# Later places in TensorE's queue for second blocks of norms, attention's transposes, one filter's products and the memory's transposes

## The chip, the cores and the metric

One core of a Trainium2 chip runs the whole program. The time is that of one execution on the device, in microseconds (us); the kernel before took 1537.53 us in the median of three runs (1534.23 to 1537.7). TensorE (PE) multiplies and transposes, VectorE (DVE) and ScalarE (ACT) do elementwise work, GpSimd (POOL) some squares, and SyncE's queue (SP) brings the weights in.

## The reference

Two networks of depth 2 run one behind the other on 256 tokens of 1024 numbers, in fp32. Each layer of the first is a mixer, a cross attention over a memory of 256 tokens and a feed-forward part, with a layer norm behind each:

```
for l in range(DEPTH):
    mix = hybrid_mixer(h, w_in[l], conv_w[l], ..., w_out[l], cos, sin)
    h = layer_norm(DEEPNORM_ALPHA * h + mix, ln1_g[l], ln1_b[l])
    h = layer_norm(DEEPNORM_ALPHA * h + cross_attention(h, mem, cq_w[l], ckv_w[l], co_w[l]),
                   ln2_g[l], ln2_b[l])
    h = layer_norm(DEEPNORM_ALPHA * h + swiglu(h, ffn_wi[l], ffn_wo[l]), ln3_g[l], ln3_b[l])
```

The mixer has two branches of one projection: a gated recurrence, and attention of 16 query heads over 2 key heads in a window of 128 tokens, with a sink per head:

```
r = jax.nn.sigmoid(... w_rg ... + b_rg)
i = jax.nn.sigmoid(... w_ig ... + b_ig)
log_a = -LRU_C * r * softplus(-lru_lambda)
h = associative_scan(combine, (exp(log_a), sqrt(-expm1(2 * log_a)) * (i * xc)))
y_rnn = h * gelu(gr)
probs = softmax(concatenate([scores, sink]))[..., :-1]
merged = sigmoid(g_rnn) * (y_rnn @ w_br_rnn) + sigmoid(g_attn) * (y_attn @ w_br_attn)
```

The second network has a differential attention and long convolutions by FFT, whose filters come from a small sine network times a decay: `h = (a @ w_out) * exp(-t * abs(deltas))`. Two layers have two filters each.

## The kernel before, in words

Every weight is used once. SyncE's queue streams them in chunks of 1 MB (`raw`, three buffers). A chunk is used in two halves; of each half ACT makes a rounded copy `wh` (L231) and DVE the remainder `wl` (L233), in four buffers each, and each product is the sum of three matmuls (`wh` with the high part of the activations, `wl` with it, `wh` with their low part). The activations are split in the same way (L360 on ACT, L361 on DVE). An `fm` tile gives features on partitions and is 48 matmuls of 256 columns; `tm` and `ff` give tokens on partitions, 512 columns a matmul; `gate` tiles, of 12 matmuls, are the two gate products of the recurrence. These four are called bulk work here: 98% of PE's time is kept by them and by the side work that stands between them.

Side work is written as coroutines. PE's and SP's queues stand in the order in which the program issues instructions. It keeps a clock of its own, `self.t`, that each matmul advances; a coroutine that says `yield L["sc"]` is not asked again until that clock has gone on by `L["sc"]` (in ns), and its next step is then issued at the next point between bulk work where such steps are let in (each 12 matmuls of 256 columns, or 6 of 512). So the table `L` sets, for each step, how much bulk work stands ahead of it on PE; it is no wait on the chip. DVE's, ACT's and POOL's queues are ordered by a scheduler, which sees PE's order, the dependences and a priority per coroutine (`PRI`). Each engine then runs its queue strictly in order.

The side work that matters:

- Attention (`swa_co`, L676 to 730). For four groups (block of 128 tokens, key head): scores `sc`; on DVE mask and maximum (L688, L692); on ACT exponentials in place (`scs`, L699), their sums' reciprocal spread out (`rbs`, L707); then `yield L["sc"]`; transposes `pt`, copied from PSUM by ACT (L717); `rb` and `y`; and a product on DVE (L729) and a split. Groups of the first block take scores in two parts. `scs` tiles have five buffers.
- The gates (L758 on). ACT takes each `gate` tile out of PSUM by two sigmoids (`r`) or two tanhs (`ig`), all L782. `fm` and `gate` tiles share a PSUM pool of four buffers; `tx`, `tm`, `sc`, `pt`, `rb`, `y` and `ff` another of four.
- The recurrence (`rnn_co`): 16 exponentials and tanhs (L803, L805), a square root (L815), gelu of the other branch (`gr`, L817), scans on DVE (L821 to L826).
- A norm's result is transposed by block of 128 tokens, eight `tx` each from `t` (written last at L601): `ln_co` issues the first block after 500 ns, the second after `L["ln<layer><norm>"]`.
- The memory's transposes (`tx` from `mem`), at the start.
- `vec_co`: transposes of small vectors, copied by DVE (L547; L1201 in a part that it calls), and rates of the recurrence (L550 to L572).
- Filters: `filter_mul` multiplies (`fh`, L1325 on) by a weight `fwo` that ACT and DVE split (L1308, L1309). Three of the four filters are late; the one at layer 0, index 1 is not.

ACT holds one set of functions at a time; where the next instruction's function is in another set, the queue has an ACT_TABLE_LOAD.

Of the kernel before, what the change touches and what calls it, by code (L numbers as in the profile page):

```python
# [38 lines left out]
LATE = ((0, 0), (1, 0), (1, 1))  # L39
# [1 line left out]
NSLOT = 29  # L41
NTMP = 8
NKEEP = 5
PRI = {'filter_dft': -60, 'cross_co': 60, 'filter_end': 30, 'rnn_co': 30, 'mlp_co': 60}

L = dict(
    vec=6000, flt=12000, fh=1200, fe=18000, prep=15000, mlp=7500, sc=11000, rnn=7000, rnn2=11700,
    pt=3000, tx=0, spec=6000, sp0=3000, sp1=5000, sp2=5000, sp3=5000, ds=9000, dn=8960, do=5500,
    z=12000, cn=1000, cp=2000, ln_0=500, ln01=3500, ln02=5500, ln03=6000, ln11=5000, ln12=4000, pre0=5100,
    pre1=5000, rope=5000, sw0=1120, sw_end=1500, sw1=1000, sw2=1500, cv0=800, cv1=1050, rnn3=1800,  # L50
    rnn_end=3000, cx0=1500, cx1=1000, cx2=800, cx_end=1500, ml=7200, fm=3000, fe0=4000, eo0=6000,
    eo1=12000, eo2=8000, fd=6000, di0=1500, dw=850, di_end=1500, c30=770, c31=1300, hy0=1300,
    hy1=2000, hy2=500, hy3=1600, hy_end=2000, pre_n=3000, pre_n1=2300, prep2=30000, mem=8700, mt=2500, vt=2500)


def shape_constants():
# [47 lines left out]
class Net:  # L104
# [28 lines left out]
    def spawn(self, gen, bg=False):  # L133
        co = Co(gen, self.t, PRI.get(gen.__name__, 0))
        (self.bg if bg else self.chains).append(co)
        return co
# [1176 lines left out]

    def filter_mul(self, l, o, hf, wos, res):
        nc = self.nc
        yield L["fm"]
        late = (l, o) in LATE
        fts = []
        for d, w in enumerate(wos):
            if late:  # L1320
                fts.append(self.slot("ft", [TB, 512]))
            for tb in range(TB):
                ps = self.pst([512], "fh")
                ts = slice(tb * P, (tb + 1) * P)
                self.mm(ps, self.a3[l][:, ts], w[:, 0], True, False)  # L1325
                self.mm(ps, self.a3[l][:, ts], w[:, 1], False, True)
                if late:
                    nc.scalar.activation(fts[d][:, tb, :], ps, AF.Copy)
                    yield 0
                else:  # L1330
                    nc.vector.tensor_tensor(hf[d][:, tb, :], ps, hf[d][:, tb, :], op=ALU.mult)
                    yield L["fh"]
        self.fco[l].append(self.spawn(self.filter_eo(l, o, hf, fts, res)))
# [488 lines left out]
```

## Time and profile before

| | |
|---|---|
| median of three runs | 1537.53 us |
| profiled execution | 1536.95 us, span 1535.1 us |
| PE, DVE, ACT, POOL busy | 98%, 71%, 56%, 5% |
| PE's granted clock, mean | 0.994 |
| DMA over the span | 172 GB/s |

Times in the profile are counted from the span's start; 1.85 us of the execution lie outside it. A row of a timeline gives the start, how long the instruction or run of like instructions took, and in brackets the idle time of its engine before it with what ended that. Matmuls overlap, so the time from one start to the next says more than a duration.

### The profile page before, as it was taken

How to read it: one execution, taken by the hardware profiler on the slowest of the kernel's cores; microseconds unless marked ns; L12 is line 12 of the kernel's file. 1: busy time of each engine (PE TensorE's matmuls, PEld its weight loads, DVE VectorE, ACT ScalarE, POOL GpSimd, SP SyncE). 2: the span in 40 equal slices, each digit the busy share in tenths (PEclk: the TensorE clock that was granted, in tenths of full speed). 3: DMA queues.
4: the chain of work that ended last, by engine and by line, in shares of the span. 5: the costliest groups of instructions: out<-in, count | busy, mean ns of one | idle time of the engine just before them, and what ended most of it. 6: DMA issues, size and time to landing. Idle time of an engine off the chain costs nothing. (4 is left out here: it accounts for less than half of the span.)

```text
span 1535.1 us, 25767 instructions
## 1 busy us (share of the span) xinstructions
PE 1501.0 (98%) x10597; PEld 1385.5 (90%) x10597; DVE 1096.0 (71%) x1591; ACT 862.0 (56%) x1338; POOL 83.8 (5%) x153
## 2 busy tenths in 40 slices
PE   9999999999999999999999999999999999999997
PEld 6889999989999989899989798999798998898996
DVE  5877667668664577858676776555897987797865
ACT  5789444545444445797445556644545655555742
POOL 4001000000000000001010010000000010000000
PEclk9999999999999999999999999999999999999999
DMA  8434655545555545436565476465355356354442
GB/s 285 138 122 154 220 193 165 187 149 203 175 174 184 192 165 164 138 122 222 192 190 195 151 244 197 167 240 192 107 159 178 112 174 211 110 170 138 165 156 79
DMA packets 202982, 263.93 MB, mean 172 GB/s; under 512 B 5491, under 2 KB 163413, under 8 KB 202864
## 3 DMA queue, kind: packets, MB, share of 16 engines
q1 hardware_dynamic: 197232, 246.43, 48.1%
q0 software_dynamic: 5632, 15.86, 3.6%
q8 instruction: 83, 1.36, 0.4%
q14 instruction: 35, 0.29, 0.1%
HBM read 261.21 MB, written 2.11 MB: 172 GB/s over the span
## 5 line engine op out<-in xcount | busy, mean ns | idle before, releaser
L233 DVE TENSOR_TENSOR wl<-raw,wh 128x1024 fp32r<-128x1024 f32 x464 | 567.1, 1226 | 294.8 <-ACT wh L231 293.0
L231 ACT ACTIVATE wh<-raw 128x1024 fp32r<-128x1024 f32 (+1 forms) x465 | 490.2, 1057 | 442.3 <-PE fm L371 244.6
L371 PE MATMUL fm<-n2h,wh 128*128 128x256 f32 x640 | 176.6, 286 | 1.0 <-ACT n2h L360 1.0
L371 PE MATMUL fm<-n2l,wh 128*128 128x256 f32 x640 | 174.7, 283 | 0.0
L371 PE MATMUL fm<-n2h,wl 128*128 128x256 f32 x640 | 174.5, 283 | 0.0
L371 PE MATMUL fm<-h2h,wh 128*128 128x256 f32 x704 | 171.6, 285 | 0.0
L371 PE MATMUL fm<-h2h,wl 128*128 128x256 f32 x704 | 171.0, 284 | 0.0
L371 PE MATMUL fm<-h2l,wh 128*128 128x256 f32 x704 | 171.0, 284 | 0.0
L371 PEld LDWEIGHTS fm<-h2h,wh 128*128 128x128 f32 x704 | 124.1, 193 | 3.4 <-issue 1.9
L371 PEld LDWEIGHTS fm<-h2h,wl 128*128 128x128 f32 x704 | 122.8, 193 | 0.1
L371 PEld LDWEIGHTS fm<-h2l,wh 128*128 128x128 f32 x704 | 122.9, 193 | 0.0
L371 PEld LDWEIGHTS fm<-n2h,wh 128*128 128x128 f32 x640 | 119.9, 192 | 3.1 <-ACT n2h L360 1.5
L371 PEld LDWEIGHTS fm<-n2l,wh 128*128 128x128 f32 x640 | 119.8, 192 | 0.4 <-DVE n2l L361 0.4
L371 PEld LDWEIGHTS fm<-n2h,wl 128*128 128x128 f32 x640 | 119.8, 192 | 0.2
L371 PE MATMUL fm<-h3h,wh 128*128 128x256 f32 x256 | 71.4, 289 | 0.0
L371 PE MATMUL fm<-xTh,wh 128*128 128x256 f32 x256 | 71.0, 288 | 0.0
L371 PE MATMUL fm<-h3h,wl 128*128 128x256 f32 x256 | 70.3, 285 | 0.0
L371 PE MATMUL fm<-h3l,wh 128*128 128x256 f32 x256 | 70.3, 285 | 0.0
L371 PE MATMUL fm<-xTh,wl 128*128 128x256 f32 x256 | 69.8, 283 | 0.0
L371 PE MATMUL fm<-xTl,wh 128*128 128x256 f32 x256 | 69.8, 283 | 0.0
L371 PE MATMUL ff<-wh,ah 128*128 128x512 f32 x176 | 68.9, 392 | 0.0
L371 PE MATMUL ff<-wl,ah 128*128 128x512 f32 x176 | 68.7, 390 | 0.0
(437 smaller groups left out, 3649.4 us busy)
## 6 DMA issues: line engine op xcount, KB each, us to landing
raw<-in_w_in_dram SPq DMA_DIRECT2D x89, 1024.0 KB, 5.2
raw<-in_ffn_wi_dram SPq DMA_DIRECT2D x44, 1024.0 KB, 5.0
raw<-in_ffn_wo_dram SPq DMA_DIRECT2D x22, 1024.0 KB, 4.8
raw<-in_w_out_dram SPq DMA_DIRECT2D x16, 1024.0 KB, 5.0
raw<-in_ckv_w_dram SPq DMA_DIRECT2D x16, 1024.0 KB, 5.3
raw<-in_w_br_attn_dram SPq DMA_DIRECT2D x8, 1024.0 KB, 5.0
raw<-in_w_br_rnn_dram SPq DMA_DIRECT2D x8, 1024.0 KB, 4.9
raw<-in_cq_w_dram SPq DMA_DIRECT2D x8, 1024.0 KB, 4.8
```

The lines of the kernel that those rows point to most:

```text
L231: hi_ins = self.nc.scalar.activation(hi[:, i:i + q], s[:, i:i + q], AF.Copy)
L233: lo_ins = self.nc.vector.tensor_tensor(lo, s, hi.bitcast(F32), op=ALU.subtract)
L371: self.nc.tensor.matmul(out, lhsT=l, rhs=r, start=start, stop=stop)
```

## The change

Numbers of the table `L` are raised, `vec_co` gets a priority, and the filter that isn't late gets a number of its own:

```diff
-PRI = {..., 'rnn_co': 30, 'mlp_co': 60}
+PRI = {..., 'rnn_co': 30, 'mlp_co': 60,
+       'vec_co': 60}
-    vec=6000, flt=12000, ..., mlp=7500, sc=11000, rnn=7000, rnn2=11700,
+    vec=6000, flt=12000, ..., mlp=7500, sc=13000, rnn=7000, rnn2=11700,
-    z=12000, ..., ln01=3500, ln02=5500, ln03=6000, ln11=5000, ln12=4000, pre0=5100,
+    z=12000, ..., ln01=5500, ln02=5500, ln03=8200, ln11=6000, ln12=4000, pre0=5100,
-    rnn_end=3000, ..., ml=7200, fm=3000, fe0=4000, eo0=6000,
+    rnn_end=3000, ..., ml=7200, fm=3000, fm1=7500, fe0=4000, eo0=6000,
-    hy1=2000, ..., prep2=30000, mem=8700, mt=2500, vt=2500)
+    hy1=2000, ..., prep2=30000, mem=10200, mt=2500, vt=2500)
@@ filter_mul
-        yield L["fm"]
+        yield L["fm"] if (l, o) in LATE else L["fm1"]
```

PE's 10,597 matmuls are the same, and bulk work keeps its order. What moves on PE: the four groups of `tx` from `mem`, by 6 matmuls of 512 columns each; in both layers' attention the transposes `pt` by 24 to 72 matmuls of 256 columns, and `rb`, `y` and the later `sc` with them, by 24 to 72; the second block's `tx` of norm 1 of layer 0 by 12 and of norm 3 of layer 0 by 24 matmuls of 256 columns, of norm 1 of layer 1 by 6 of 512; the four groups of `fh` of the filter that isn't late, from inside an `fm` tile to `ff` tiles and the next `fm` tile. SP's and POOL's queues stand as they stood, but for one small load that POOL issues one place later. DVE has the same instructions in another order around attention, ACT eight more ACT_TABLE_LOADs, 37 where there were 29: four in each layer's mixer. The line numbers of the kernel after are one higher, by the added line.

TensorE at the gates of layer 0, before. Numbers behind names tell tiles apart; `xch` and `xcl` are the two parts of the gates' input.

```order
621 L371 MATMUL gate_1370<-xch_1351,wh_1236 128x256
622 L371 MATMUL gate_1370<-xcl_1352,wh_1236 128x256
623 L371 MATMUL gate_1370<-xch_1351,wl_1237 128x256
624 L383 MATMUL rb_1389<-ident,rbs_1174 128x128 x4
625 L371 MATMUL y_1395<-pt_1142,kv_271 64x512 x2
626 L383 MATMUL pt_1401<-ident,scs_1202 128x128 x4
627 L383 MATMUL pt_1407<-ident,scs_1205 128x128 x4
628 L371 MATMUL gate_1413<-xch_1347,wh_1265 128x256
629 L371 MATMUL gate_1413<-xcl_1348,wh_1265 128x256
```

The third group's `rb` and `y` and the fourth group's `pt` stand behind the second gate tile; the third group's `pt` came 48 matmuls earlier. TensorE in the same place, after:

```order
643 L372 MATMUL gate_1392<-xch_1339,wh_1155 128x256
644 L372 MATMUL gate_1392<-xcl_1340,wh_1155 128x256
645 L372 MATMUL gate_1392<-xch_1339,wl_1156 128x256
646 L384 MATMUL pt_1413<-ident,scs_1214 128x128 x4
647 L384 MATMUL pt_1419<-ident,scs_1217 128x128 x4
648 L372 MATMUL gate_1433<-xch_1425,wh_1296 128x256
649 L372 MATMUL gate_1433<-xcl_1426,wh_1296 128x256
650 L372 MATMUL gate_1433<-xch_1425,wl_1297 128x256
651 L372 MATMUL gate_1433<-xch_1425,wh_1296 128x256
```

Now it is the third group's `pt`, behind the fourth gate tile (tiles 1343, 1358, 1377 and 1392 stand ahead, then come 1433, 1448, 1467 and 1482); the fourth group's `pt` has gone behind all eight.

ScalarE's queue for the same gate tiles, before: first the last exponentials, then a table load and every sigmoid and tanh.

```order
113 L699 ACTIVATE scs_1205,sst_1191<-scs_1205,sst_1191 128x128 x4
114 L703 ACTIVATE sst_1191<-sst_1191 128x8
115 L782 ACT_TABLE_LOAD
116 L782 ACTIVATE r_1343<-gate_1355,v_0_450 128x256
117 L707 ACTIVATE rbs_1222<-sst_1191 128x512
118 L782 ACTIVATE r_1343<-gate_1355,v_0_450 128x256
119 L782 ACTIVATE r_1343<-gate_1370,v_0_450 128x256 x2
120 L231 ACTIVATE wh_1385<-raw_1099 128x1024
121 L717 ACTIVATE pt_1190<-pt_1401 128x512
122 L722 ACTIVATE rbs_1174<-rb_1389 128x512
123 L717 ACTIVATE pt_1190<-pt_1407 128x512
124 L782 ACTIVATE ig_1345<-gate_1413,hb_452 128x256 x2
```

ScalarE's queue for the same gate tiles, after:

```order
110 L783 ACT_TABLE_LOAD
111 L783 ACTIVATE r_1331<-gate_1343,v_0_450 128x256 x2
112 L783 ACTIVATE r_1331<-gate_1358,v_0_450 128x256 x2
113 L232 ACTIVATE wh_1373<-raw_1085 128x1024
114 L700 ACT_TABLE_LOAD
115 L700 ACTIVATE scs_1262,sst_1251<-scs_1262,sst_1251 128x128 x4
116 L700 ACTIVATE scs_1265,sst_1251<-scs_1265,sst_1251 128x128 x4
117 L704 ACTIVATE sst_1251<-sst_1251 128x8
118 L783 ACTIVATE ig_1333<-gate_1377,hb_452 128x256 x2
119 L708 ACTIVATE rbs_1282<-sst_1251 128x512
120 L783 ACTIVATE ig_1333<-gate_1392,hb_452 128x256 x2
121 L232 ACTIVATE wh_1407<-raw_1085 128x1024
```

The fourth group's exponentials now stand behind the first two gate tiles' sigmoids and ahead of the third tile's tanhs, with a table load on each side; a third load, for tile 1433's sigmoids, stands at place 124.

TensorE at norm 3 of layer 0, before: `tx` of the second block in the middle of the last `fm` tile.

```order
3396 L371 MATMUL fm_5897<-memTh_226,wl_5809 128x256
3397 L371 MATMUL fm_5897<-memTl_228,wh_5808 128x256
3398 L383 MATMUL tx_5926<-ident,t_3958 128x128 x4
3399 L383 MATMUL tx_5933<-ident,t_3958 128x128 x4
3400 L371 MATMUL fm_5897<-memTh_225,wh_5812 128x256
3401 L371 MATMUL fm_5897<-memTh_225,wl_5813 128x256
```

TensorE in the same place, after (`h3h` and `h3l` are the split of that `tx`, one tile for both blocks; `tm_5972` is the first block's product, `tm_5973` the second's):

```order
3420 L372 MATMUL fm_5897<-memTh_226,wl_5813 128x256
3421 L372 MATMUL fm_5897<-memTl_228,wh_5812 128x256
3422 L384 MATMUL tx_5958<-ident,t_3958 128x128 x4
3423 L384 MATMUL tx_5965<-ident,t_3958 128x128 x4
3424 L372 MATMUL tm_5972<-wh_5861,h3h_5818 128x512
3425 L372 MATMUL tm_5972<-wl_5862,h3h_5818 128x512
3426 L372 MATMUL tm_5972<-wh_5861,h3l_5820 128x512
3427 L372 MATMUL tm_5972<-wh_5861,h3h_5818 128x512
3428 L372 MATMUL tm_5972<-wl_5862,h3h_5818 128x512
3429 L372 MATMUL tm_5972<-wh_5861,h3l_5820 128x512
3430 L372 MATMUL tm_5973<-wh_5861,h3h_5818 128x512
3431 L372 MATMUL tm_5973<-wl_5862,h3h_5818 128x512
```

The second block's `tx` has moved to the end of the `fm` tile, and one `tm` group of the first block stands between it and its first user. The first block's `tx`, 36 matmuls ahead of the `fm` tile shown, stands where it stood.

## Rows read from the trace of the kernel before

**Rows 1.** The page: busy time of each engine over the span.

```profile
PE 1501.0 (98%) x10597; PEld 1385.5 (90%) x10597; DVE 1096.0 (71%) x1591; ACT 862.0 (56%) x1338; POOL 83.8 (5%) x153
```

**Rows 2.** Timeline of PE where the moved steps stand; start, us, idle in brackets.

```profile
23.88 0.63 PE L383 MATMUL tx<-ident,mem 128*128 128x128 f32 x4 [0.97 <-DMA mem<-in_mem_dram]
...
247.05 1.32 PE L383 MATMUL tx<-ident,t 128*128 128x128 f32 x8 [1.22 <-DVE t L601]
...
554.32 1.32 PE L383 MATMUL tx<-ident,t 128*128 128x128 f32 x8 [1.40 <-DVE t L601]
...
562.67 1.04 PE L383 MATMUL tx<-ident,t 128*128 128x128 f32 x8
...
801.90 0.66 PE L383 MATMUL tx<-ident,t 128*128 128x128 f32 x4 [0.54 <-DVE h1l L361]
...
922.74 0.50 PE L371 MATMUL fh<-fwo,a 128*128 128x512 f32 x1 [1.00 <-ACT fwo L1308]
923.47 0.50 PE L371 MATMUL fh<-fwo,a 128*128 128x512 f32 x1 [0.22 <-DVE fwo L1309]
```

**Rows 3.** Timeline of PE at the vectors' transposes.

```profile
50.56 1.53 PE L383 MATMUL qt<-ident,q 128*128 128x128 f32 x12 [1.41 <-DVE v L1201]
```

**Rows 4.** Timeline of ACT ahead of it.

```profile
48.42 1.28 ACT L568 ACT_TABLE_LOAD   x1
```

**Rows 5.** Timeline of DVE at norm 3 of layer 0.

```profile
564.01 2.36 DVE L233 TENSOR_TENSOR wl<-raw,wh 128x1024 fp32r<-128x1024 f32 x2
566.28 1.29 DVE L361 TENSOR_TENSOR h3l<-tx,h3h 128x512 fp32r<-128x512 f32 x2
```

**Rows 6.** Busy time of engines at layer 0's gates: stretch, PE, PEld, DVE, ACT, POOL, PE's clock, DMA.

```profile
119.00:124.00 5.00, 5.00 (x39) 4.02 (x38) 4.38 (x6) 5.00 (x13) 0.00 (x0) 1.00 0.01 3
```

**Rows 7.** Timeline of PE from layer 0's third group to its gates.

```profile
90.96 0.60 PE L383 MATMUL rb<-ident,rbs 128*128 128x128 f32 x4
...
97.01 1.47 PE L371 MATMUL sc<-kv,qT 64*128 64x128 f32 x16
...
109.44 0.28 PE L371 MATMUL gate<-xch,wh 128*128 128x256 f32 x1
...
112.28 0.60 PE L383 MATMUL rb<-ident,rbs 128*128 128x128 f32 x4
...
113.81 1.09 PE L383 MATMUL pt<-ident,scs 128*128 128x128 f32 x8
114.66 0.36 PE L371 MATMUL gate<-xch,wh 128*128 128x256 f32 x1
```

**Rows 8.** Timeline of ACT at layer 0's gates and recurrence.

```profile
110.13 1.05 ACT L231 ACTIVATE wh<-raw 128x1024 fp32r<-128x1024 f32 x1
111.08 0.39 ACT L699 ACTIVATE scs<-scs,sst 128x128 f32<-128x128 f32 x1
...
114.37 1.28 ACT L782 ACT_TABLE_LOAD   x1
115.67 0.47 ACT L782 ACTIVATE r<-gate,v 128x256 f32<-128x256 f32 x1
116.04 0.62 ACT L707 ACTIVATE rbs<-sst 128x512 f32<-128x512 f32 x1
116.56 1.20 ACT L782 ACTIVATE r<-gate,v 128x256 f32<-128x256 f32 x3
...
133.41 0.90 ACT L803 ACTIVATE xc<-r,rates 128x256 f32<-128x256 f32 x2
```

**Rows 9.** Timeline of PE in layer 1's attention.

```profile
640.35 2.17 PE L383 MATMUL pt<-ident,scs 128*128 128x128 f32 x8 [1.89 <-ACT scs L699]
...
644.87 0.69 PE L383 MATMUL rb<-ident,rbs 128*128 128x128 f32 x4
```

**Rows 10.** Busy time and clock in that place; columns as in rows 6.

```profile
642.00:644.00 2.00, 2.00 (x10) 2.00 (x11) 0.27 (x2) 2.00 (x5) 0.00 (x0) 0.50 0.49 163
```

**Rows 11.** ACT's exponentials by shape: count, busy us, mean ns, idle before.

```profile
L699 ACT ACTIVATE scs<-scs,sst 128x256 f32<-128x256 f32 x32 | 15.9, 498 | 9.8 <-DVE sst L695 9.7
L699 ACT ACTIVATE scs<-scs,sst 128x128 f32<-128x128 f32 x32 | 12.4, 389 | 0.0
```

More of the change, by code (lines that the diff above doesn't have):

```diff
@@ L43 @@
 NKEEP = 5
-PRI = {'filter_dft': -60, 'cross_co': 60, 'filter_end': 30, 'rnn_co': 30, 'mlp_co': 60}
+PRI = {'filter_dft': -60, 'cross_co': 60, 'filter_end': 30, 'rnn_co': 30, 'mlp_co': 60,
+       'vec_co': 60}
 L = dict(
-    vec=6000, flt=12000, fh=1200, fe=18000, prep=15000, mlp=7500, sc=11000, rnn=7000, rnn2=11700,
+    vec=6000, flt=12000, fh=1200, fe=18000, prep=15000, mlp=7500, sc=13000, rnn=7000, rnn2=11700,
     pt=3000, tx=0, spec=6000, sp0=3000, sp1=5000, sp2=5000, sp3=5000, ds=9000, dn=8960, do=5500,
-    z=12000, cn=1000, cp=2000, ln_0=500, ln01=3500, ln02=5500, ln03=6000, ln11=5000, ln12=4000, pre0=5100,
+    z=12000, cn=1000, cp=2000, ln_0=500, ln01=5500, ln02=5500, ln03=8200, ln11=6000, ln12=4000, pre0=5100,
     pre1=5000, rope=5000, sw0=1120, sw_end=1500, sw1=1000, sw2=1500, cv0=800, cv1=1050, rnn3=1800,
-    rnn_end=3000, cx0=1500, cx1=1000, cx2=800, cx_end=1500, ml=7200, fm=3000, fe0=4000, eo0=6000,
+    rnn_end=3000, cx0=1500, cx1=1000, cx2=800, cx_end=1500, ml=7200, fm=3000, fm1=7500, fe0=4000, eo0=6000,
     eo1=12000, eo2=8000, fd=6000, di0=1500, dw=850, di_end=1500, c30=770, c31=1300, hy0=1300,
-    hy1=2000, hy2=500, hy3=1600, hy_end=2000, pre_n=3000, pre_n1=2300, prep2=30000, mem=8700, mt=2500, vt=2500)
+    hy1=2000, hy2=500, hy3=1600, hy_end=2000, pre_n=3000, pre_n1=2300, prep2=30000, mem=10200, mt=2500, vt=2500)
 def shape_constants():
```

## The prediction

> **What bounds the kernel now.** I read the page first: PE is busy 98% of the span, DVE 71%, ACT 56% [rows 1]. So time can only be won where PE stands idle, and the reader is to see how little that is. I then read PE's waits and the timeline at each step that moves. Six idle stretches touch a moved step: 0.97 us for the memory's DMA, 1.22 and 1.40 us for a norm's `t` and 0.54 us for `h1l`, 1.00 and 0.22 us for `fwo` [rows 2], 1.41 us for DVE's copy of a vector [rows 3] and 1.89 us for exponentials in layer 1's attention [rows 9]. Behind the last one PE ran at half its clock: 0.50 of 2.4 GHz, that is 1.2, from 642 to 644 us [rows 10]. The price of that stall with its slow clock: from 638.46 (640.35 less 1.89) to 644.87 PE did 8 transposes and 12 `fm` matmuls [rows 9]. Eight transposes take 0.85 us (113.81 to 114.66 [rows 7]) and 12 matmuls 1.42 (24 took 2.84 from 109.44 to 112.28 [rows 7]), in all 2.3 where 6.4 went by: 4.1 us lost. Last I looked at who else is near its limit: at layer 0's gates ACT is busy all of 119 to 124 us [rows 6]. An engine that has 56% over the span has nothing left there.
>
> **What the moves remove.** A step that waited and is moved later by more bulk work than it waited loses the wait.
> - Memory: 6 matmuls of 512 columns, some 1.4 us, cover 0.97: -1.0. The transposed memory is first used in the cross attention, behind the whole mixer, so nothing is late.
> - Norm 1 of layer 0: 12 matmuls, 1.4 us, cover 1.22: -1.2, and its eight `tx`, which take more than the 0.85 of rows 7 because they start between DVE's two halves of `t`, give back 0.2. Its first user stands a tile and more later.
> - Norm 1 of layer 1: 6 matmuls of 512 cover 0.54: -0.5. The split behind it has two tiles' `wl` ahead of it on DVE; by their 1.14 us each [rows 5] it ends 0.3 us before its first user. Cover thin, but there.
> - `fh`: moved past the rest of its tile: -1.2; what a `fh` pair costs stays. Its products go into filters of the second network, so nothing near waits for them.
> - Norm 3 of layer 0: the order shows that the pair which waited 1.40 us at 554.32 is the first block's and stays; the second block's, at 562.67, waited for nothing [rows 2]. So nothing goes, and something comes: after the change one `tm` group, 1.36 us, stands between the `tx` and its first user. ACT must first do the last `fm` tile's copy and one `wh`, 0.5 and 0.95 us by the starts of rows 8, and DVE a `wl` of 1.14 and `h3l` of 0.6 [rows 5]. From the end of the `fm` tile that is about 3.3 us, against 0.8 for the `tx`, 1.4 for the group and 0.45 for two matmuls: +0.7. Bounds 0 (DVE free at once) and +1.3.
> - `vec_co`: the copy that held up `qt` keeps its place in DVE's queue. It stands behind the second layer's rates, and these wait for ACT, which spends 48.42 to 49.70 on a table load [rows 4]. A priority on DVE can't shorten that: 0, bounds -0.2 and +0.2.
>
> Sum without attention: -1.0 - 1.4 - 0.5 - 1.2 + 0.7 = -3.4.
>
> **Attention, layer 0.** No stall of a size worth naming stands here before, so only costs can come. PE in the new order, on the clock of before: the third group's scores stand 48 `fm` matmuls later. Before, the block of two `rb`, `y` and scores begins at 90.96 and its last `y` ends at 97.01 [rows 7]; 48 matmuls at 0.12 are 5.8, so this `y` ends at 102.8. With 1.4 for the last scores, 36 `fm` matmuls (4.4), four gate tiles (5.7), `pt` (0.85) and two more tiles (2.85) PE wants tile 1467 at 118.0. That tile takes the PSUM of tile 1377, which ACT's tanhs release.
>
> ACT gets to the third group's exponentials when the last `y` has been through DVE (0.6) and a split of 0.5, at 104.0. From there its queue has, with the starts of rows 8: three table loads of 1.30 (114.37 to 115.67), 3.9; sixteen exponentials of 0.39, 6.2; three `wh` of 0.95, 2.85; `gr` and `rbs` of 0.5, 1.0; two small ones, 0.2; four sigmoids of 0.36, 1.4; two tanhs of the same size, 0.7. That is 16.3, so the release comes at 120.3 and PE waits 2.3 us. Before, the same exponentials ended ahead of all sigmoids, under one load, and no wait was seen. Bounds: 0, if ACT's start is 2.3 us earlier than I have it, and 3.3, if each `wh` and `y` comes late by the little that such rows vary.
>
> What is behind it: ACT goes on without a gap, so the lag is handed down. The fourth group's `y` waits for copies of `pt` (+0.35). The `wh` that the second tile behind it needs stands behind a load and 16 exponentials and tanhs of 0.40 (133.41, two in 0.80 [rows 8]); its `wl` comes 1.0 late. Two more table loads between the square roots push the scans, and DVE has a `wl` behind scans: +1.2, bounds 0 and 2. Layer 0: 2.3 + 0.35 + 1.0 + 1.2 = +4.9.
>
> A half clock after the 2.3 us stall, as in rows 10, would cost PE up to 1.7 us, but PE then only comes later to waits that ACT and DVE set anyway. I take 0.
>
> **Attention, layer 1.** The same order. The 4.1 us go, since 24 to 72 matmuls cover 1.89. But the second half of the first block's exponentials now has gelu and two table loads ahead of it (2.6 + 0.95): 0.5 us each [rows 11], they end 1.1 us after PE wants them, the second pair another 0.5: +1.6. Copies of `pt` then hold up `y` and scores, +0.7. The gates wait again, 1.6 here, since PE comes later and ACT has one load less ahead; +0.4 and +2.2 behind it as in layer 0. 1.6 + 0.7 + 1.6 + 0.4 + 2.2 - 4.1 = +2.4.
>
> **The sum.** -3.4 + 4.9 + 2.4 = +3.9. The profiled execution took 1536.95, 1.85 outside its span, so the kernel after comes to 1540.9; it lay 0.6 below the median of 1537.53, well inside the runs' spread. I say 1540.5, since thin waits of 0.3 to 0.5 us among the terms may vanish.
>
> **A rule that speaks against the change.** After the load at 114.37 (1.28 long) the sigmoid starts at 115.67, 0.02 us behind it [rows 8]. The Trainium skill (ScalarE: Activation LUTs, What ACT_TABLE_LOAD costs) puts a switch at 1283 ns and a drain of 1380 more, and advises to finish one set of functions before the next. Its load agrees with the row, its drain does not show there. By its figure each load would cost 2.66, and three of them would make layer 0's gate wait 6.4 instead of 2.3.
>
> **The rivals.**
> - ACT keeps pace (faster). If the exponentials overlap the sigmoids without holding up a tile, all that remains of attention is layer 1's -4.1: 1536.95 - 3.4 - 4.1 = 1529.5; with half the waits some 1535. For it: before, no `pt` of layer 0's gates waited (113.81 has no idle time [rows 7]). Against it: ACT has no gap there that three more loads could go into [rows 6].
> - The half clock bites (slower). Each of three new stalls near 2 us drops the clock as the 1.89 us one did [rows 10]. If PE and not ACT is then the later one, that is up to 1.7 each: 1540.9 + 3 x 1.7 = 1546, and 1543 with one or two. [...]
> - A load drains ACT (slower): a wait of 4.1 us more at the gates of either layer, 1549. Rows 8 speak against it; it would need loads that follow PSUM work to behave otherwise than this one. This is the rule above.
> - The change doesn't do what it says: so for `vec_co` and norm 3, within the sum already; for attention the order shows that it does.
>
> **How the numbers follow.** My forecast, 1540.5 with 1536 to 1544 as its own range, 0.50; ACT keeps pace 0.23; half clock 0.22; drained loads 0.05. What this kernel's runs can tell from no change is about 0.3%, 4.6 us: below 1532.9 is faster, above 1542.1 slower. Of the forecast 0.33 falls within, 0.15 above, and 0.02 below, if the late waits on `wl` vanish; of ACT keeping pace 0.18 below and 0.05 within; of the half clock 0.02 within and 0.20 above; drained loads all above, 0.05. So faster 0.20, same 0.40, slower 0.40. The range goes from 1530, the first rival's full case, to 1547, the second's.
>
> **What would show it.** Right, if the waits named in rows 2 for the memory, for norm 1 of both layers and for `fwo` are gone, `qt` still waits 1.4 us and the first block of norm 3 1.4 us; if in either layer's mixer a `gate` tile waits 1.5 to 3 us for ACT's tanhs with eight exponentials between two table loads ahead of them; if a `tm` behind norm 3 waits 0.7 us for `h3l`; and if two `fm` tiles in each layer wait about 1 us for `wl`. Wrong, if no gate tile waits: then ACT reached them earlier than my sum, and the time is near 1530. Wrong the other way, if PE's clock shows 0.50 for several microseconds at both layers' gates and the time exceeds 1546.

## The result, and the profile after

The kernel after takes 1548.82 us (median of 4 runs, 1547.4 to 1549.83), the kernel before beside it 1537.37 (4 runs, 1534.23 to 1537.7). The ratio is 1.0075, with a 95% interval of 1.0063 to 1.0087: slower by 11.4 us. Predicted were 1540.5 us, and a range that ends at 1547. The profiled execution took 1547.4 us.

The page of the kernel after, its span and its busy times:

```profile
span 1545.6 us, 25759 instructions
PE 1504.6 (97%) x10597; PEld 1387.3 (90%) x10597; DVE 1096.7 (71%) x1591; ACT 871.9 (56%) x1346; POOL 84.1 (5%) x153
```

Beside [rows 1], ACT has 8 instructions more, all of them table loads, and 9.9 us more busy time. PE has the same 10,597 matmuls.

PE's waits in the kernel after: line and tile, the releaser, us in all, how often, and the longest.

```profile
PE gate L372 <- ACT ig L783: 6.6, 2, 3.9
PE tx L384 <- DVE t L602: 4.7, 3, 3.0
...
PE fm L372 <- DVE wl L234: 3.1, 4, 0.9
...
PE qt L384 <- DVE v L1202: 1.4, 1, 1.4
...
PE pt L384 <- ACT scs L700: 0.9, 1, 0.9
...
PE tm L372 <- DVE h3l L362: 0.6, 1, 0.6
```

The waits of [rows 2] for the memory's DMA, for `h1l` and for `fwo` are gone, and one of those for `t`; that of `qt` [rows 3] and the 1.40 us of norm 3's first block stay. The gates, which waited for nothing before, now wait 6.6 us, and four `fm` tiles wait for `wl`.

The timeline of PE in the kernel after, at the places of [rows 7] and [rows 9] and at norm 3 of layer 0 (start, us, then the instruction; in brackets the idle time ahead of it):

```profile
95.88 0.66 PE L384 MATMUL rb<-ident,rbs 128*128 128x128 f32 x4 [0.42 <-ACT pt L718]
...
100.63 1.95 PE L372 MATMUL y<-pt,kv 128*64 128x512 f32 x8
...
117.67 0.28 PE L372 MATMUL gate<-xch,wl 128*128 128x256 f32 x1
121.85 0.58 PE L372 MATMUL gate<-xch,wh 128*128 128x256 f32 x1 [3.91 <-ACT ig L783]
...
575.61 0.51 PE L372 MATMUL tm<-wh,h3l 128*128 128x512 f32 x1 [0.64 <-DVE h3l L362]
...
652.57 1.42 PE L384 MATMUL pt<-ident,scs 128*128 128x128 f32 x6 [0.87 <-ACT scs L700]
...
680.54 0.39 PE L372 MATMUL gate<-xch,wh 128*128 128x256 f32 x1 [2.73 <-ACT ig L783]
```

Busy time and PE's clock behind the two gate waits in the kernel after (columns as in [rows 6]):

```profile
118.00:120.00 2.00, 0.00 (x0) 0.00 (x0) 0.00 (x0) 2.00 (x11) 0.00 (x0) 1.00 0.51 178
...
122.00:124.00 2.00, 2.00 (x10) 2.00 (x11) 1.22 (x2) 2.00 (x5) 0.00 (x0) 0.50 0.00 0
124.00:126.00 2.00, 2.00 (x14) 2.00 (x14) 1.22 (x1) 1.98 (x3) 0.00 (x0) 0.68 0.00 0
...
682.00:684.00 2.00, 2.00 (x11) 2.00 (x11) 1.68 (x2) 1.98 (x4) 0.00 (x0) 0.50 0.00 0
```

The first row is the picture of the loss: for 2 us PE did nothing and ACT was busy throughout. Then PE came back at 0.50 of its 2.4 GHz, that is at 1.2.

To see where time was lost and won, I lined up the 9,456 matmuls of bulk work in the two traces, which stand in the same order, and took the differences of their starts:

| stretch | predicted, us | trace after less before, us |
|---|---|---|
| memory | -1.0 | -1.2 |
| attention and gates, layer 0 | +4.9 | +9.2 |
| norm 1, layer 0 | -1.4 | -1.4 |
| norm 3, layer 0 | +0.7 | +1.1 |
| attention and gates, layer 1 | +2.4 | +5.4 |
| norm 1, layer 1 | -0.5 | -0.9 |
| `fh` | -1.2 | -1.7 |
| all else | 0 | -0.2 |
| sum | +3.9 | +10.3 |

What the moves remove came out as forecast or up to 0.5 us better; norm 3 costs 0.4 more than forecast. The two attention terms are each about twice their forecast.

### The profile page after: what moved, and what is told of

It is laid out like the page before. It is cut to its first block, busy times and chain, and to the rows that moved or that the text cites. A ratio compares the mean times of both kernels' runs of the same rounds, so it can differ in the third digit from the quotient of the medians.

```text
span 1545.6 us, 25759 instructions
## 1 busy us (share of the span) xinstructions
PE 1504.6 (97%) x10597; PEld 1387.3 (90%) x10597; DVE 1096.7 (71%) x1591; ACT 871.9 (56%) x1346; POOL 84.1 (5%) x153
```

## The experiments

The kernel before was run beside each group of experiments: medians 1537.45, 1537.22 and 1537.03 us. One trace can differ from another by 3.4 us in the first 55 us alone (experiments 8 and 9, whose kernels are alike up to layer 1), so times are medians and the traces are compared within a stretch.

**1. Attention's number alone.**

```diff
 (kernel before)
-    ... mlp=7500, sc=11000, ...
+    ... mlp=7500, sc=13000, ...
```

(`fm1` is in this kernel too, at the old 3000.)

> The kernel before with the attention's wait alone raised (sc 13000), all else as it was. My theory: the whole loss stands in the two layers' attention and gates; between the same bulk matmuls the traces of before and after part by +9.2 us in layer 0 and +5.4 us in layer 1, so this kernel is 14.6 us slower than before, some 1552 us, and each layer shows a gate tile waiting 2.7 to 4 us for the tanhs, with PE at half its clock for 3.4 us behind it. Rival: the parts act on each other (norms and products that come later meet the attention's backlog), and the attention alone costs what the prediction said, +7.3 us: 1544.7.

1551.51 us (1550.05 to 1553.54), ratio 1.0093 [1.008, 1.0107]: +14.1. One number of the table costs more than the whole change. By the lined-up traces it loses 9.2 us in layer 0 and 5.4 in layer 1, as the whole change does, and its gates wait 3.91 and 2.73 us, as there. One part of the forecast did not come: behind layer 1's gate wait PE's clock stayed at 1.00. Busy time and clock there:

```profile
684.00:686.00 2.00, 2.00 (x19) 1.94 (x17) 1.74 (x2) 1.98 (x4) 0.00 (x0) 1.00 0.00 0
```

Yet layer 1 loses the same 5.4 us as in the kernel after, where the clock fell to 0.50.

**2. Everything but attention.**

```diff
 (kernel after)
-    ... mlp=7500, sc=13000, ...
+    ... mlp=7500, sc=11000, ...
```

> The kernel after with the attention's wait put back (sc 11000). My theory: the moves outside attention keep the gains that the traces show (memory -1.0 to -1.4, norm 1 of layer 0 -1.5, norm 1 of layer 1 -1.0, the filter's products -1.7, norm 3 +1.2), about -4.2 us: 1533 us, and the 1.89 us wait of layer 1 with its half clock is back. Rival: gains of about 1 us ahead of a later wait are given back there (DMA or DVE set the pace), 0 to -2: 1536 to 1537.5.

1532.51 us (1531.54 to 1533.13), ratio 0.9967 [0.9955, 0.9979]: -4.9. With experiment 1 that makes +9.2, where the whole change has +11.4; the runs' spread allows for the difference.

**3. Also without norm 3 and the priority.**

```diff
 (kernel of experiment 2)
-PRI = {..., 'mlp_co': 60, 'vec_co': 60}
+PRI = {..., 'mlp_co': 60}
-    ... ln03=8200, ...
+    ... ln03=6000, ...
```

> As the run with all but attention, and norm 3 of layer 0 and the vectors' priority put back too. My theory: norm 3's second block waited for nothing before and its move costs 1.2 us (0.64 idle and slower groups around it), the priority does nothing: 1.2 us faster than the run with all but attention, some 1532. Rival: what norm 3 adds is hidden by the slack behind it, no difference within 0.3 us; or the priority earns its 1.4 us, then this one is slower than that run.

1532.02 us (1531.1 to 1534.8), ratio 0.9968 [0.9956, 0.9981]. The `tm` that waited 0.64 us for `h3l` waits no more in its trace, and the 1.1 us that norm 3 costs in experiment 2's trace is gone; `qt` waits 1.42 us in both traces. But 0.5 us between medians is less than the runs' spread: by time it is not resolved.

**4. The gate wait filled with work that nobody needs.** Twelve matmuls of 512 columns stand where the gates wait, so that PE has work there.

```diff
 (kernel after, gates)
+            if h == 1 and which == 1:
+                dm = self.pch([512], "dm")
+                for _ in range(12):
+                    nc.tensor.matmul(dm, lhsT=self.wm[:, :P], rhs=self.wm, start=True, stop=True)
```

> The kernel after with 12 more matmuls of 512 columns (bf16, results unused), some 2.6 us, put on PE between the sixth and the seventh gate tile of each layer, where PE waits 3.9 and 2.7 us for ACT. They change nothing but PE's idle time. Theory that the half clock behind this wait costs 1.6 us a layer and isn't hidden: the clock stays at 1.00 there and the kernel is 2 to 3.3 us faster than the kernel after, 1545.5 to 1547. Rival (the prediction's own step): PE only comes earlier to waits that ACT and DVE set, so 0 to -0.5 us although the clock stays up; or +, if 12 matmuls are longer than the wait.

1548.05 us (1546.65 to 1549.89), ratio 1.0071 [1.0058, 1.0084]: 0.8 below the kernel after, which is within the spread. Busy time and clock of this kernel in layer 0, and PE's waits from 85 to 180 us:

```profile
120.00:122.00 2.00, 0.73 (x4) 0.12 (x2) 0.38 (x3) 2.00 (x10) 0.00 (x0) 1.00 0.00 0
122.00:124.00 2.00, 1.99 (x16) 1.99 (x17) 1.38 (x2) 2.00 (x4) 0.00 (x0) 1.00 0.00 0
```

```profile
PE fm L372 <- DVE wl L234: 1.8, 2, 0.9
PE gate L372 <- ACT ig L787: 1.3, 1, 1.3
...
PE fm L372 <- ACT wh L232: 0.4, 1, 0.4
```

The clock now stays at 1.00, and six matmuls into the second tile behind the wait PE is 1.4 us ahead of the kernel after. But 0.6 of that is gone behind the fourth group's `rb` and `y`, the `fm` tile at 141 us takes 7.5 us where it took 6.6, and the tile behind it starts at 148.68 us in this trace and at 148.56 in that of the kernel after. So the half clock is seen, yet it isn't what the time hangs on: what PE gains by the full clock it hands back, mostly waiting for ACT's `wh` and DVE's `wl`. In either layer the lined-up traces of this kernel and of the kernel after lose the same within 0.1 us, and experiment 1's layer 1, where the clock did not fall, says so too.

**5. One table load more.**

```diff
 (kernel after, gates)
+                if (h, which, i) == (0, 1, 0):
+                    nc.scalar.activation(self.tiny(1, "ge"), ps[:, 0, 0:1], AF.Gelu_apprx_tanh)
                 for m in range(2):
```

> The changed kernel with one thing more: ahead of the first input gate's tanhs of either layer ACT does one gelu on a single column of the same PSUM tile (its result is used by nobody), which brings one table load more ahead of the release of the gates' PSUM (39 loads instead of 37); PE's and DVE's order are the changed kernel's. Theory (ACT is the path from the third group's exponentials to the recurrence, so that what is added to its queue there goes to the end): 1.28 for the load and some 0.2 for the gelu, so the gate waits go from 3.9 to 5.4 and from 2.7 to 4.2 us, and the time rises by 2.4 to 3.4 us, to about 1551.8. Rival (the waits at the gates are mostly absorbed by later ones, as the half clock behind them was): the gate waits grow as said, but the time rises by less than 1 us.

1550.37 us (1549.35 to 1551.26), ratio 1.0086 [1.0072, 1.0099]: 1.6 above the kernel after. ACT and PE's waits of this kernel, first of layer 0, then of layer 1:

```profile
120.25 1.28 ACT L782 ACT_TABLE_LOAD   x1
121.54 0.17 ACT L782 ACTIVATE ge<-gate 128x1 f32<-128x1 f32 x1
121.61 0.62 ACT L708 ACTIVATE rbs<-sst 128x512 f32<-128x512 f32 x1
122.13 1.56 ACT L785 ACTIVATE ig<-gate,hb 128x256 f32<-128x256 f32 x4
```

```profile
PE gate L372 <- ACT ig L785: 5.9, 1, 5.9
PE fm L372 <- DVE wl L234: 0.9, 1, 0.9
...
PE gate L372 <- ACT ig L785: 4.7, 1, 4.7
PE fm L372 <- DVE wl L234: 0.9, 1, 0.9
```

Each gate wait grows by 2.0 us: the load and the gelu as expected, and 0.5 for an `rbs` that now stands ahead of the tanhs. By the lined-up traces 1.5 us of that in either layer reach the end of the mixer; one of the two waits for `wl` goes in exchange. The sum of 2.9 fits the theory, the 1.6 between medians lies between it and the rival, and the intervals don't separate them, nor this kernel from the kernel after.

**6. The r gates without the sigmoid.**

```diff
 (kernel after)
-            g, b, func, scale = ((s.r, self.vec1(l, "b_rg"), AF.Sigmoid, 1.0),
+            g, b, func, scale = ((s.r, self.half_rg[l], AF.Tanh, 0.5),
...
-        nc.vector.tensor_scalar(sp, ab, 8.0, None, op0=ALU.mult)
+        nc.vector.tensor_scalar(sp, ab, 4.0, None, op0=ALU.mult)
...
-                                     scale=sp[:, c:c + 1])
+                                     scale=sp[:, c:c + 1], bias=sp[:, c:c + 1])
```

(and `nsp` likewise; `half_rg` is half of `b_rg`.)

> The changed kernel with the r gates computed as 0.5 + 0.5 tanh(x/2) instead of by the sigmoid, the halves folded into the rates, so that they need no table load between exponentials and tanhs: 30 loads instead of 37; PE's order is the changed kernel's. In layer 0 ACT now does all gates with no load between them and ahead of the last eight exponentials; in layer 1 a gelu with its two loads lands between them. Theory (what ACT has to do ahead of the gates' release sets the time, loads above all): layer 0's release has two loads and eight exponentials less ahead of it, 2.6 + 3.1 us, so its gate wait of 3.9 goes, with the half clock and most of the 2.3 us of waits for wl behind it; layer 1's release still has two loads ahead of it, so that its wait stays at 2.7 to 3.3, and only the waits behind it shrink by up to 2.3. Time 1537.5 to 1541. Rival (the later scores themselves cost the time, and the loads hide behind them): both gate waits stay, time above 1547.

1541.03 us (1539.86 to 1542.98), ratio 1.0025 [1.0014, 1.0036]: 7.8 below the kernel after, with the same order on PE. Its trace has one gate wait left, that of layer 1 (timeline of PE); busy time and clock at layer 0's gates stand behind it, then two of PE's waits from 85 to 180 us:

```profile
679.77 0.39 PE L372 MATMUL gate<-xch,wh 128*128 128x256 f32 x1 [2.96 <-ACT ig L786]
```

```profile
118.00:126.00 8.00, 7.69 (x58) 6.35 (x57) 3.16 (x8) 8.00 (x28) 0.00 (x0) 1.00 0.79 257
```

```profile
PE fm L372 <- DVE wl L234: 1.8, 2, 0.9
...
PE fm L372 <- ACT wh L232: 0.4, 1, 0.4
```

For the gates the forecast holds: where the loads ahead of the release went, the wait of 3.91 us and the slow clock went; where two loads stayed, 2.96 us stayed. It fails for layer 0's waits for `wl`, most of which were to go: they took 1.5 us in the kernel after and take 1.8 here. By the lined-up traces layer 0 wins 4.3 us and layer 1 2.0. In layer 0 eight exponentials (3.1 us) also moved behind the release, so this run doesn't price the loads alone; experiment 5 does. 1541.03 is the upper edge of what I expected; the last section names a cost that I had not counted.

**7. The same in the kernel before.** The edit of experiment 6.

> The kernel before, with the r gates by tanh in the same way: no load between exponentials, r gates and input gates in either layer (29 loads in all as before, since other places need one more). Theory (a load costs only where ACT is waited for): PE waited for nothing at these gates before, so the time stays within 2 us of the kernel before, 1536 to 1538.5. Rival (each load in attention costs its 1.28 us wherever it stands): four loads less there, 1532.3.

1537.83 us (1535.48 to 1539.85, 11 runs), ratio 1.0004 [0.9995, 1.0013]: no difference. Two loads in each layer have left the gates and two stand between the recurrence's square roots instead, 29 in all as before, and PE waits for neither place. So a load taken from the gates wins nothing in the order in which PE doesn't wait for what stands behind it; what one load less in all is worth there, this run doesn't show.

**8 to 10. Only what gains.** To the kernel of experiment 3 come later places for the two steps that did wait: norm 3's first block (all three kernels), and layer 1's last `pt` of its second block (by 1500 ns in experiment 8, 900 in 9, not in 10).

```diff
-        yield L["ln_0"]
+        first = 2000 if (l, i) == (0, 3) else L["ln_0"]
+        yield first
         yield from self.to_fm_block(t, hT, 0)
-        yield L[f"ln{l}{i}"] - L["ln_0"]
+        yield L[f"ln{l}{i}"] - first
...
-                yield L["sc"]
+                yield L["sc"] + (1500 if (l, kv, tb, r0) == (1, 1, 1, 2) else 0)
```

> The parts of the change that removed a wait (memory, norm 1 of both layers, filter half), attention's wait as before, norm 3 and the vectors as before, and two edits in the sense of the change: norm 3's first block of transposes in layer 0 is due 1500 ns later (that is the one that waited 1.40 us), and of attention's scores only layer 1's last ones of the second block are due 1500 ns later, those that made PE wait 1.89 us and run at half its clock. Theory: the third experiment's 1532.0 less 1.4 for norm 3 less up to 4.1 for layer 1, since 29 table loads stay: 1526.5 to 1529. Rival (new waits of the same size take their place, as in the changed kernel's attention): 1531 to 1534.

> The eighth experiment's kernel with one number changed: layer 1's last scores of the second block are due 900 ns later instead of 1500. In PE's order only 12 fm matmuls (1.4 us) then change places with these transposes, where 1500 ns moved them past the next block's scores. Theory (a move should be as long as the wait and pass nothing that others wait for): of the 1.9 us stall 0.5 is left, the clock does not fall behind it, and of the 4.1 us some 2.5 to 3.5 are won where the eighth experiment's trace shows 1.3: 1527 to 1529. Rival (rb and y, which now follow the transposes at once, wait for ACT's copies of pt and take it back): 1530 to 1531.

> As the ninth, with layer 1's scores as before: the third experiment's kernel and norm 3's first block of layer 0 due 1500 ns later, nothing else. Theory: its stall of 1.40 us is covered by one tm group of 1.4 us and its h3l stands far enough ahead, so 1.2 us less than the third experiment's 1532.0: 1530.8. Rival (the stall moves to the user of h3l, as it did for the second block in the changed kernel): 1532 to 1532.5.

| | us | ratio to before |
|---|---|---|
| 8 | 1529.83 (1529.22 to 1531.06) | 0.9955 [0.9941, 0.9968] |
| 9 | 1529.5 (1528.38 to 1531.86) | 0.9953 [0.9941, 0.9965] |
| 10 | 1530.86 (1529.89 to 1532.47) | 0.9961 [0.9949, 0.9973] |

Norm 3 in experiment 10 (timeline of PE), and layer 1's attention in experiments 8 and 9 (waits of PE, two of 8, then two of 9):

```profile
551.74 1.32 PE L383 MATMUL tx<-ident,t 128*128 128x128 f32 x8
...
564.63 0.50 PE L371 MATMUL tm<-wh,h3l 128*128 128x512 f32 x1 [0.25 <-DVE h3l L361]
```

```profile
PE pt L383 <- DVE rbs L730: 0.9, 1, 0.9
PE pt L383 <- ACT rbs L723: 0.8, 1, 0.8
```

```profile
PE pt L383 <- ACT scs L700: 0.5, 1, 0.5
PE sc L371 <- ACT rbs L723: 0.3, 1, 0.3
```

Experiment 10's median is as expected, 1.2 below experiment 3, though their intervals overlap: the 1.40 us are covered, 0.25 come at `h3l`, and in the lined-up traces norm 3 wins 0.9. Experiment 8 passed the next block's `rb`, `y` and scores, and two new waits took the place of the old one, in sum 1.7 where 1.9 stood; behind them PE's clock fell to 0.50 (644 to 646 us). Its time lies between the theory and the rival. Experiment 9 leaves 0.5 of the stall with no slow clock behind it, as expected; but from the start of the next `y` to the scores go 2.25 us instead of 1.88, since the scores wait for ACT's `rbs`. The rival had such a wait ahead of `rb` and `y`, where none is. In the lined-up traces layer 1 wins 2.2 us, between medians 1.4, less than the 2.5 to 3.5 expected. 8 and 9 can't be told apart by time. Both beat the kernel before by 7 us and the kernel after by 19.

## Why the prediction was wrong

**What held.** The mechanism: ACT's exponentials between two loads, ahead of the tanhs that release the gates' PSUM, in both layers. PE wanted tile 1467 at 117.95 (118.0 in the sum). The sum without attention, -3.4, is -4.9 in experiment 2. `qt` and norm 3's first block kept their waits, norm 3's second block got one of 0.64 (0.7 forecast, 1.1 in the lined-up traces), and four `fm` tiles wait for `wl`. The rival in which ACT keeps pace is out.

**The step that failed: when ACT starts, and so the gates' terms of 2.3 and 1.6.** They measured 3.91, above the bound of 3.3, and 2.73. In layer 0 the queue that I counted behind the start, 16.3 us, took 16.6 (105.17 to the end of the tanhs at 121.8). But it started at 105.17 and not at 104.0. In the sum the last `y` went through DVE as soon as it was done. It was done at 102.58 (100.63 and 1.95 above), and DVE was not free. DVE, then ACT, in the kernel after, from there to the gates' release (the rows of ACT answer to [rows 8]):

```profile
100.81 0.69 DVE L362 TENSOR_TENSOR yal<-rbs,yah 128x512 fp32r<-128x512 f32 x1 [0.70 <-ACT yah L361]
101.42 1.28 DVE L689 SCALAR_TENSOR_TENSOR scs<-sc,mask 128x512 f32<-128x512 f32 x2
102.62 1.27 DVE L693 TENSOR_REDUCE sst<-scs 128x4 f32<-128x512 f32 x2
103.80 0.68 DVE L730 TENSOR_TENSOR rbs<-y,rbs 128x512 f32<-128x512 f32 x1
```

```profile
104.52 0.63 ACT L361 ACTIVATE yah<-rbs 128x512 fp32r<-128x512 f32 x1 [3.12 <-DVE rbs L730]
105.17 1.28 ACT L700 ACT_TABLE_LOAD   x1
...
112.67 1.28 ACT L783 ACT_TABLE_LOAD   x1
113.97 1.57 ACT L783 ACTIVATE r<-gate,v 128x256 f32<-128x256 f32 x4
...
116.50 1.28 ACT L700 ACT_TABLE_LOAD   x1
117.80 0.40 ACT L700 ACTIVATE scs<-scs,sst 128x128 f32<-128x128 f32 x1
...
120.99 0.81 ACT L783 ACTIVATE ig<-gate,hb 128x256 f32<-128x256 f32 x2
```

The `y` product stood behind masks and maxima of the next scores, which themselves stood behind the split of the `y` before, and that waited for ACT. So DVE took the product 1.2 us late, while ACT stood idle for 3.12 us. In layer 1 DVE takes the product at once (at 662.96; `y` is done at 662.83), but the last maximum of the next scores stands behind the product, and the exponentials wait for what DVE makes of it (`sst`):

```profile
665.16 0.40 ACT L700 ACTIVATE scs<-scs,sst 128x128 f32<-128x128 f32 x1 [0.84 <-DVE sst L696]
```

From there to the end of the tanhs at 680.5 ACT takes 15.3 us, where the 16.3 of the sum less one load of 1.30 are 15.0. So in both layers the sum left out what DVE does for the scores between the last `y` and ACT's start. This is read from the trace; no experiment moved it.

**The lag behind the gates, taken as 2.2 and 0.35 or 0.4, is 3.9 in either layer.** In the kernel after it shows as 1.6 us of half clock and some 2.3 of tiles that wait for `wl`. Experiment 4 shows that these are one quantity: without the half clock the waits grow by about as much. ACT has no idle time above 0.1 us from 104.52 to 164.5 us in the kernel after, and from the load at 105.17 to the `wh` at 161.00 it takes 55.83 us; in experiment 4, with PE at full clock, it takes 55.80. So the step "a half clock ... I take 0" was right as a mechanism, and what the sum had too small is how far ACT and DVE lag there. Without a half clock over them the terms can be read in experiment 4's layer 0: some 0.6 at the fourth group's `y` (0.35 in the sum), 1.8 at the tile at 141 us (1.0), 1.4 at the tiles behind it (1.2). Why ACT and DVE are that much later there stays open.

**Left out:** in layer 0 copies of `pt` stand behind gelu and its load, so that `rb` waits 0.42 and scores wait for PSUM, about 1.0 in all. The sum priced this in layer 1 only (2.3, measured 2.8). Tile 1433, which waits for ACT's sigmoids of the first tiles, is another 0.4.

Layer 0 is then 1.0 + 0.4 + 4.1 (the gate wait by the tile's length) + 3.9 = 9.4, where the lined-up traces have 9.2; layer 1 is 2.8 + 2.9 + 3.9 - 4.1 = 5.5 against 5.4. Of what the two layers' sums lack, the gates' terms are some 3 us, the lag 2.7 and the earlier waits 1.9.

**What the loads have to do with it.** Experiment 6 does with 30 loads instead of 37, with the same order on PE, and wins 7.8 us; experiment 7 moves the loads away from the same gates where nobody waits, and wins nothing; experiment 5 adds one per layer and shows 1.28 us for it, with the next instruction 0.01 us behind. The Trainium skill (ScalarE: Activation LUTs, Table sets: the hidden batching unit) advises to batch activation calls by set, and that is what the change undid. The Trainium skill (ScalarE: Activation LUTs, What ACT_TABLE_LOAD costs) puts a drain of 1380 ns to each switch; none shows in these rows. So the rival of drained loads has the right side for another reason. Its 1549 us came nearest, but by waits of 6.4 us that no gate had. The rival of the half clock gave 1546 by a clock that did fall, and by a cost that neither experiment 4 nor experiment 1's layer 1 shows.

What stays open: how the remaining 8.5 us between experiments 6 and 2 divide. By the lined-up traces 4.9 lie in layer 0's mixer and 3.8 in layer 1's. Layer 1's gate wait of 2.96 is in it, the early waits and layer 0's waits for `wh` and `wl`; I did not take them away one by one.

## What to carry to other kernels

A step that is moved on the busiest engine also moves what it triggers: before a due time is raised, write out the queue of the engine that works for it, with table loads and with what its input must pass on a third engine. Move a step only if it waited, by about as much as it waited, and past nothing that others wait for. And before a clock that falls behind a stall is called a loss, look at whether the next wait takes it back.

## What was not expected of the hardware

- The same stall with and without a slow clock. Late in the program an `fd` matmul waits 3.1 us in all twelve traces. In seven of them PE's granted clock falls to 0.50 within 2 us behind it (in four the first matmul already runs at about half speed), in five it stays at 1.00. Before, then after:

```profile
1085.85 0.79 PE L371 MATMUL fd<-foh,dft 128*128 128x512 f32 x1 [3.10 <-ACT ft L1328]
```

```profile
1096.46 0.50 PE L372 MATMUL fd<-foh,dft 128*128 128x512 f32 x1 [3.14 <-ACT ft L1329]
```

The 48th matmul behind this one starts 9.5 us later in the five and 10.1 to 11.5 in the seven. So a trace can owe 0.7 to 2 us to this place alone, and idle time alone doesn't tell whether the clock falls. Other stalls say the same: a gate wait of 2.96 us in experiment 6 and the 1.89 us of layer 1's `pt` in experiment 7 have 1.00 behind them, and `qt`'s 1.42 us in experiment 9 has 0.50, where the same wait in the kernel before had 1.00.

- In these runs a bias column beside a scale column makes an ACT instruction longer. The recurrence's exponentials take 498 ns in the kernel after; with the bias of experiments 6 and 7 they take 652 and 596. These are ACT's groups in the kernel after and in experiment 7:

```profile
L804 ACT ACTIVATE xc<-r,rates 128x256 f32<-128x256 f32 x16 | 7.4, 498 | 0.0
```

```profile
L806 ACT ACTIVATE xc<-r,rates 128x256 f32<-128x256 f32 x16 | 9.0, 596 | 0.0
```

For 16 exponentials and 16 tanhs that is 3 to 4 us of ACT's busy time (each group is busy 9.0 or 9.5 us instead of 7.4), which experiment 6 paid out of what it saved in loads.
